# Both attentions of a two-layer diffusion block with the query halves in the two row halves of TensorE

## The chip, the core and the metric

The kernel runs on one core of a Trainium2 chip. The metric is the device time of one execution in microseconds. The kernel before takes 1738.92 us, the median of three runs (1737.24 to 1739.38). The profiled execution that all readings below come from spans 1736.6 us, 2.3 us less than that median. The names of engines in the profile: PE is TensorE's matmul, PEld its weight load, DVE VectorE, ACT ScalarE, POOL GpSimd, SP the engine that issues the transfers.

## The reference

Two layers work on 1024 latent tokens and 256 context tokens of width 1024. Each has an adaLN-modulated RMSNorm, an attention, a SiLU gate and an output projection. Layer 0 is grouped-query attention, 16 query heads of 64 on 4 key heads; layer 1 is latent attention, 16 heads whose query and key have 64 plain and 32 rotary dimensions, the rotary key shared by all heads. Cut to what matters here:

```
s = einsum('bqhgd,bkhd->bhgqk', q, k) * 64 ** -0.5          # layer 0
s = (einsum('bqhd,bkhd->bhqk', q_nope, k_nope)
     + einsum('bqhr,bkr->bhqk', q_rope, k_rope)) * 96 ** -0.5   # layer 1
p = softmax(s, axis=-1)
o = einsum('bhqk,bkhd->bqhd', p, v)
```

Latent queries see 1280 keys (1024 latent and 256 context). In layer 0 the context queries are computed too, over the 256 context keys; layer 1 gives out latent tokens only.

## The kernel before, in words

The program goes through layer 0's projections, layer 0's attention, its output projection with layer 1's norm, layer 1's projections, layer 1's attention, and its output projection. Everything that has to be exact is split into a high and a low part of the 4-byte type `F32R` (names ending in H and L, or A and B), and a product is a sum of high x high, low x high and high x low.

**An attention unit.** `Attention.run` goes over units, one head each (16 latent units in each layer; layer 0 also has four short units, one for the context queries of each key group). A unit has ten key tiles of 128 keys. For each key tile `do_scores` makes a score tile `st` of 128 keys x 1024 queries, in two matmuls of 512 queries for each product (line 422), and ACT takes its exponential into `p` (line 424). The unit ends with `do_av`, which multiplies `p` by the values with two matmuls side by side, one for each query half, in the two column halves of the array (line 458), and with `total`, the softmax sum, a matmul in four column quarters (line 500).

- Layer 0's scores are two products: `KA` (128 rows: the high key above the low key) with `QA` (the high query twice), and `KB` (64 rows of the high key and a row of -1) with `QB` (the low query and the row `crow` of maxima).
- Layer 1's are three: 96 rows of the high key with the low query, 96 of the low key with the high query, and 97 with the high parts of both and the row of maxima.

**The maxima.** The softmax subtracts a maximum per query. It is found ahead of the scores: for the unit after this one, 20 steps each make a tile `mx` of 128 queries x 512 keys with a matmul (16 steps with latent keys, kind "lat", one matmul of 512 columns at line 362; four steps with the context keys, kind "ctx", two of 256 columns at line 367 for two query tiles), and DVE reduces the tile (lines 363 and 369). After the 20th step `do_shift` reduces once more; its `turn` transposes the maxima on PE at the end of the running unit's scores, DVE copies them into `crow`, and SP sends them into the last row of the next unit's query tile. Two steps stand between the matmuls of each key tile. The first steps (28 in layer 0, 24 in layer 1) are made earlier, between the projection matmuls of the gate (`gate_slice`, lines 92 to 94).

**What sets the order.** In `run`, the instructions of PE, DVE and ACT stand in the order in which the code records them; POOL's and SP's are placed by the framework's scheduler. In the gate stage ahead of it, the scheduler places PE's too. PE's, DVE's and ACT's instructions start in the order of their queues. A tile is made again from a ring: `mx` has two PSUM banks, `st` two pairs of banks, `av` two. POOL adds up the `p` tiles for the softmax sum; DVE adds the last four in pairs (`pair_sum`, line 431) after the unit's scores.

## Time and profile before

| | |
|---|---|
| median of three runs | 1738.92 us |
| span of the profiled execution | 1736.6 us |
| PE busy | 1703.1 us (98%), 8548 matmul records |
| PEld busy | 1232.5 us (71%) |
| DVE busy | 1068.4 us (62%) |
| ACT, POOL busy | 644.5 us (37%), 979.5 us (56%) |
| TensorE clock granted | 0.997 |
| layer 0's attention, first score to last values | 367.9 to 763.3 us |
| layer 1's attention, first score to last sum | 1196.9 to 1645.0 us |

A busy time is the time in which at least one instruction of the engine ran. A matmul's own duration in the records is longer than the time it holds the array, since matmuls follow each other in a pipeline: what a matmul costs is the distance from its start to the next one's. In a timeline a row is a run of equal instructions: start, length, engine, line, what is written and read, shape, count, and in brackets the idle time before it with what ended it. The shape `96*128 96x512` is 96 rows and 128 columns of weights, and 512 columns that stream.

### The profile page before, as it was taken

The numbers are of one execution on the slowest core, as the hardware profiler recorded it, in microseconds if no ns is written. First come the engines' busy times: TensorE is split into PE (matmuls) and PEld (weight loads), VectorE is DVE, ScalarE is ACT, GpSimd is POOL, SyncE is SP. The second block draws the span as 40 slices with busy tenths as digits, with TensorE's granted clock in tenths as the row PEclk, the third lists the DMA queues.
The fourth block names the chain that finished last, engine by engine and source line by source line (L and its number), as shares of the span: only waits on it lengthen the run. The fifth ranks groups of instructions, "written<-read, shape, count | busy, mean of one in ns | idle before, by whom it ended". The sixth has DMA issues, their size and how long they took to land. (4 is left out here: it accounts for less than half of the span.)

```text
span 1736.6 us, 23794 instructions
## 1 busy us (share of the span) xinstructions
PE 1703.1 (98%) x8548; PEld 1232.5 (71%) x8548; DVE 1068.4 (62%) x1807; ACT 644.5 (37%) x943; POOL 979.5 (56%) x657
## 2 busy tenths in 40 slices
PE   8999999999999999999989999999999999999998
PEld 5776778776655665558878798978666666657587
DVE  3765651368777877625575667756676767667231
ACT  4632221134544544433244633332343443434310
POOL 2763430237888897752344644443587878777511
PEclk9999999999999999999999999999999999999999
DMA  9457854432332422156434857685434443441452
GB/s 326 156 160 235 265 167 136 133 98 55 100 91 71 116 66 74 44 145 189 137 94 132 238 163 199 181 234 162 104 88 118 108 104 91 111 112 43 118 162 73
DMA packets 211901, 234.33 MB, mean 135 GB/s; under 512 B 20680, under 2 KB 157880, under 8 KB 211784
## 3 DMA queue, kind: packets, MB, share of 16 engines
q1 hardware_dynamic: 211360, 232.71, 47.2%
q8 instruction: 67, 1.10, 0.3%
q14 instruction: 50, 0.41, 0.1%
q10 hardware_dynamic: 424, 0.11, 0.0%
HBM read 158.98 MB, written 73.63 MB: 134 GB/s over the span
## 5 line engine op out<-in xcount | busy, mean ns | idle before, releaser
L363 DVE TENSOR_REDUCE m<-mx 128x1 f32<-128x512 f32 x512 | 351.5, 691 | 203.6 <-PE mx L362 201.5
L424 ACT ACTIVATE p<-st 128x1024 f32<-128x1024 f32 x328 | 335.3, 1024 | 219.5 <-PE st L422 185.1
L445 POOL TENSOR_TENSOR acp<-acp,p 128x1024 f32<-128x1024 f32 x128 | 305.7, 2388 | 8.7
L458 PE MATMUL av<-p,v 128*64 128x512 f32 x1312 | 289.9, 595 | 0.0
L458 PEld LDWEIGHTS av<-p,v 128*64 128x64 f32 x1312 | 90.8, 137 | 181.0 <-issue 178.6
L445 POOL TENSOR_TENSOR acp<-p 128x1024 f32<-128x1024 f32 x34 | 81.3, 2391 | 168.3 <-ACT p L424 167.9
L445 POOL TENSOR_TENSOR acp<-acp,acd 128x1024 f32<-128x1024 f32 x60 | 141.5, 2358 | 22.2 <-DVE acd L431 19.4
L431 DVE TENSOR_REDUCE acd<-p 128x512 f32<-128x1024 f32 x124 | 144.6, 1219 | 7.7 <-ACT p L424 7.7
L135 POOL TENSOR_TENSOR wb<-wraw,wa 128x512 fp32r<-128x512 f32 (+3 forms) x73 | 95.5, 1324 | 90.6 <-ACT wa L156 90.0
L92 PE MATMUL mm<-wa,hh 128*128 128x512 f32 (+2 forms) x336 | 127.3, 379 | 1.7 <-ACT hh L787 1.7
L422 PE MATMUL st<-QH,KL 96*128 96x512 f32 x320 | 123.5, 392 | 0.0
L94 PE MATMUL mm<-wa,hl 128*128 128x512 f32 (+2 forms) x336 | 121.3, 361 | 1.4 <-DVE hl L790 1.4
L93 PE MATMUL mm<-wb,hh 128*128 128x512 f32 (+2 forms) x336 | 120.9, 360 | 0.0
L479 ACT COPY os<-av 128x512 f32<-128x512 f32 x36 | 21.1, 586 | 252.9 <-PE av L458 173.5
L369 DVE TENSOR_REDUCE m<-mx 128x2 f32<-128x512 f32 x144 | 99.3, 692 | 25.3 <-PE mx L367 24.4
L92 PE MATMUL y<-wa,oh 128*128 128x512 f32 (+1 forms) x296 | 114.1, 386 | 0.0
L93 PE MATMUL y<-wb,oh 128*128 128x512 f32 (+1 forms) x296 | 113.6, 384 | 0.0
L94 PE MATMUL y<-wa,ol 128*128 128x512 f32 (+1 forms) x296 | 113.6, 384 | 0.0
L422 PE MATMUL st<-QA,KA 128*128 128x512 f32 x336 | 106.6, 399 | 0.7 <-ACT p L424 0.7
L422 PE MATMUL st<-QB,KB 65*128 65x512 f32 x336 | 105.5, 395 | 0.0
L362 PE MATMUL mx<-KA,QA 128*128 128x512 f32 x256 | 102.4, 405 | 1.2 <-DVE m L363 1.0
L362 PE MATMUL mx<-KH,QH 96*128 96x512 f32 x256 | 102.3, 401 | 0.0
(232 smaller groups left out, 3423.4 us busy)
## 6 DMA issues: line engine op xcount, KB each, us to landing
mraw<-in_l_w_mod SPq DMA_DIRECT2D x64, 256.0 KB
wraw<-in_l_w_in SPq DMA_DIRECT2D x28, 512.0 KB
rb<-rrow SPq DMA_DIRECT2D x72, 128.0 KB
mraw<-in_l_w_mod SPq DMA_DIRECT2D x16, 512.0 KB
sgd<-gth SPq DMA_DIRECT2D x32, 256.0 KB
QA<-q0h SPq DMA_DIRECT2D x32, 256.0 KB
wraw<-in_l_w_out SPq DMA_DIRECT2D x16, 512.0 KB
sg<-sgd SPq DMA_DIRECT2D x64, 128.0 KB
```

Source lines behind the costliest of these rows:

```text
L92: pe.matmul(ps, lhsT=lh(k), rhs=rh(k), start=first and i == 0, stop=False)
L93: pe.matmul(ps, lhsT=lh(k), rhs=rl(k), start=False, stop=False)
L94: pe.matmul(ps, lhsT=ll(k), rhs=rh(k), start=False, stop=last and i == len(ks) - 1)
L135: eng.tensor_sub(lo, a, b)
L362: pe.matmul(m, lhsT=s["mq"][:, i * P:(i + 1) * P], rhs=s["mk"][:, n * 512:(n + 1) * 512], start=True, stop=True)
L363: dve.reduce_max(s["m"][:, i, n:n + 1], m, axis=AX.X)
L369: dve.reduce_max(s["m"][:, 2 * i:2 * i + 2, 2 if u["kind"] == "lat" else 0], m.rearrange("p (a b) -> p a b", a=2), axis=AX.X)
L422: pe.matmul(ps[:, n * 512:(n + 1) * 512], lhsT=lh, rhs=rf(n), start=(j == 0), stop=(j == len(prods) - 1))
L424: act.activation(p, ps, AF.Exp, scale=self.ops["scale"])
L431: dve.reduce_sum(t[:, ns], p2.rearrange("p a n -> p n a")[:, ns, :], axis=AX.X)
L445: pool.tensor_add(t, a, b)
L458: pe.matmul(s["av"][64 * n:64 * n + 64, :], lhsT=s["v"][:, kt, u["vc"]:u["vc"] + 64], rhs=p[:, n * 512:(n + 1) * 512], start=kt == kts[0], ...
```

## The change

`HALVES` switches both layers. The array's 128 rows are used as two halves of 64: every score and maximum matmul has at most 64 rows, and the first 512 queries' lie in rows 0 to 63, the last 512 queries' in rows 64 to 127. The keys are loaded twice, once into each half of the partitions; the query tiles become 128 x 512, with one query half in each half of the partitions.

- Layer 0's scores are four products for each query half (high key x high query, low key x high query, high key x low query, and a row of -1 with the row of maxima, in tiles that are zero elsewhere); a maximum is one product of 64 rows.
- Layer 1's scores are five for each half (high, low x high, high x low, the shared rotary key's high and low part with the high rotary query, and 33 rows with the low rotary query and the maxima); a maximum is two products, plain and rotary.
- `side_by_side` records the two halves' matmuls in turn, and `scores_by_halves` puts one maximum step of each half into every key tile: half 0's ahead of its products, half 1's in the middle of its own.
- `mx` gets three banks and `av` one, so `total` goes to an `mx` tile. Layer 1's low parts (`KL`, `QL`, `QS`) get two buffers and are loaded by `rest`, at the end of the unit two before; the tile `KS` is opened when layer 1's gate stage has ended; that stage's ring of gate tiles goes from four to two.

Three places in PE's order. First layer 1's scores, one key tile with latent maxima. Names are written<-streamed,weights. Before:

```order
L422 MATMUL st<-QH,KH 128x512 x2
L362 MATMUL mx<-KH,QH 128x512
L422 MATMUL st<-QL,KH 128x512 x2
L422 MATMUL st<-QH,KL 128x512
L362 MATMUL mx<-KH,QH 128x512
L422 MATMUL st<-QH,KL 128x512
```

and with the change, where the rows of the two halves take turns:

```order
L393 MATMUL mx<-KH,QH 128x512
L501 MATMUL st<-QH,KH 128x512
L393 MATMUL mx<-KR,QR 128x512
L501 MATMUL st<-QH,KL 128x512
L501 MATMUL st<-QH,KH 128x512
L501 MATMUL st<-QL,KH 128x512
L501 MATMUL st<-QH,KL 128x512
L393 MATMUL mx<-KH,QH 128x512
L501 MATMUL st<-QL,KH 128x512
L393 MATMUL mx<-KR,QR 128x512
L501 MATMUL st<-QR,KR 128x512 x2
L501 MATMUL st<-QS,KS 128x512 x2
```

Eight matmuls of the whole array for a key tile have become fourteen of half of it. Second, a key tile of layer 1 with context maxima, with the change:

```order
L403 MATMUL mx<-KH,QH 128x256
L403 MATMUL mx<-KR,QR 128x256
L403 MATMUL mx<-KH,QH 128x256
L403 MATMUL mx<-KR,QR 128x256
L501 MATMUL st<-QH,KH 128x512
L501 MATMUL st<-QH,KL 128x512
L501 MATMUL st<-QH,KH 128x512
L501 MATMUL st<-QL,KH 128x512
L501 MATMUL st<-QH,KL 128x512
L403 MATMUL mx<-KH,QH 128x256
L403 MATMUL mx<-KR,QR 128x256
```

The four matmuls of a context step stand in one piece, all in one half. Third, the maxima in layer 1's gate stage (the `mm` rows are the gate's). Before:

```order
L362 MATMUL mx<-KH,QH 128x512 x2
L92 MATMUL mm<-hh,wa 128x512
L93 MATMUL mm<-hl,wa 128x512
L94 MATMUL mm<-hh,wb 128x512
L362 MATMUL mx<-KH,QH 128x512
```

and with the change:

```order
L393 MATMUL mx<-KH,QH 128x512 x2
L393 MATMUL mx<-KR,QR 128x512 x2
L393 MATMUL mx<-KH,QH 128x512
L393 MATMUL mx<-KR,QR 128x512
L93 MATMUL mm<-hh,wa 128x512
L393 MATMUL mx<-KH,QH 128x512
L393 MATMUL mx<-KR,QR 128x512
L94 MATMUL mm<-hl,wa 128x512
```

The first two maxima stand side by side, the others alone between matmuls of the whole array. The diff, cut to its core:

```diff
+HALVES = (True, True)
...
-            self.ps_m = st.enter_context(tc.tile_pool(name=f"psm{l}", bufs=2, space=PSUM, side="right", reuse_waits="tile"))
+            self.ps_m = st.enter_context(tc.tile_pool(name=f"psm{l}", bufs=3 if HALVES[l] else 2, space=PSUM, side="right", reuse_waits="tile"))
+            if HALVES[l]:
+                self.ops["open"](self, st)
...
+            if l and HALVES[l]:
+                self.ops["open_late"](self, stp)
...
+                bufs = 1 if HALVES[l] and name == "ps_o" else 2
...
+        def max_parts(self, u, step):
+            s = self.state[id(u)]
+            kind, i, n = step
+            if kind == "lat":
+                half, spans = i // 4, [(i % 4, slice(n * 512, n * 512 + 512), slice(0, 512))]
+            else:
+                half, spans = i // 2, [(2 * (i % 2) + a, slice(NL, NT), slice(a * 256, a * 256 + 256)) for a in range(2)]
+            held = {}
+            def part(j):
...
+                q, k = pairs[j]
+                for t, ks, cs in spans:
+                    pe.matmul(held["m"][:, cs], lhsT=q[:, t * P:(t + 1) * P], rhs=k[:, ks], start=j == 0, stop=j == len(pairs) - 1)
+                if j == len(pairs) - 1:
+                    dve.reduce_max(s["m"][:, i, n:n + 1], held["m"], axis=AX.X)
+            def part_ctx():
...
+                for t, ks, cs in spans:
+                    for j, (q, k) in enumerate(pairs):
+                        pe.matmul(m[:, cs], lhsT=q[:, t * P:(t + 1) * P], rhs=k[:, ks], start=j == 0, stop=j == len(pairs) - 1)
...
+            if kind == "ctx":
+                return half, [part_ctx] + [lambda: None] * (self.ops["mparts"] - 1)
+            return half, [lambda j=j: part(j) for j in range(self.ops["mparts"])]
...
-                sp.dma_start(raw(s["crow"]), raw(r))
+                if HALVES[self.l]:
+                    for n in range(2):
+                        sp.dma_start(raw(s["crow"][n]), raw(r[4 * n:4 * n + 4, :]))
...
+        def side_by_side(*streams):
+            for t in range(max(map(len, streams))):
+                for stream in streams:
+                    if t < len(stream):
+                        stream[t]()
...
+        def scores_by_halves(self, u, kt, p, steps):
...
+            streams = [[lambda j=j, n=n: product(j, n) for j in range(last + 1)] for n in range(2)]
+            for half, parts in steps:
+                at_ = (last + 2) // 2 if half else 0
+                streams[half][at_:at_] = parts
+            self.side_by_side(*streams)
+            act.activation(p, ps, AF.Exp, scale=self.ops["scale"])
...
+                            if HALVES[self.l]:
+                                count += 2
+                                self.scores_by_halves(u, kt, ps[i], self.next_maxima(count, t + 1 + ahead))
...
+                        if end and t + 2 < self.started:
+                            self.state[id(self.units[t + 2])].pop("rest", lambda: None)()
...
+    def l0_maxima(s, n):
+        r = slice(64 * n, 64 * n + 64)
+        return [(s["QH"][r, :], s["KH"][r, :])]
...
+            return [(s["KH"][r, ks], s["QH"][r, :]), (s["KL"][r, ks], s["QH"][r, :]),
+                    (s["KH"][r, ks], s["QL"][r, :]), (s["minus"][r, :], s["X"][r, :])]
...
+    def l1_open_late(at, st):
+        at.KS = st.enter_context(tc.tile_pool(name="rope1s", bufs=1, reuse_waits="tile")).tile([P, NT], F32R, name="KS")
+        for n in range(2):
+            pool.memset(raw(at.KS[64 * n + 32:64 * n + 33, :]), -1.0)
+            sp.dma_start(raw(at.KS[64 * n:64 * n + 32, :]), kr1h)
...
+        def rest():
...
+            for b, cs in halves:
+                sp.dma_start(raw(KL[b:b + 64, :]), k1l[h // 2, r, :])
+                sp.dma_start(raw(QL[b:b + 64, :]), q1l[h, 0:64, cs])
+                sp.dma_start(raw(QS[b:b + 32, :]), q1l[h, 64:96, cs])
...
+    def l1_maxima(s, n):
+        r = slice(64 * n, 64 * n + 64)
+        return [(s["QH"][r, :], s["KH"][r, :]), (s["QR"][r, :], s["KR"][r, :])]
...
+            return [(s["KH"][r, ks], s["QH"][r, :]), (s["KL"][r, ks], s["QH"][r, :]), (s["KH"][r, ks], s["QL"][r, :]),
+                    (s["KR"][r, ks], s["QR"][r, :]), (at.KS[r33, ks], s["QS"][r33, :])]
...
-    with tc.tile_pool(name="wkg1", bufs=4, **right) as wkg:
+    with tc.tile_pool(name="wkg1", bufs=2 if HALVES[1] else 4, **right) as wkg:
```

More of the change, by code (lines that the diff above doesn't have):

```diff
@@ L411, in maxima, with product @@
                     self.do_shift(u)
+        def scores_by_halves(self, u, kt, p, steps):
+            s = self.state[id(u)]
+            ps = self.ps_s.tile([P, 1024], F32, name="st", tag="st")
+            prods = [self.ops["scores"](s, kt, n) for n in range(2)]
+            last = len(prods[0]) - 1
+            def product(j, n):
+                lh, rh = prods[n][j]
+                pe.matmul(ps[:, n * 512:(n + 1) * 512], lhsT=lh, rhs=rh, start=j == 0, stop=j == last)
+            streams = [[lambda j=j, n=n: product(j, n) for j in range(last + 1)] for n in range(2)]
[4 more added lines that the diff above has]
+            act.activation(p, ps, AF.Exp, scale=self.ops["scale"])
         def do_scores(self, u, kt, p, between):
@@ L496, in total @@
             def total():
-                t = s["av"] if u is not self.units[-1] else self.ps_m.tile([P, 512], F32, name="mx", tag="mx")
+                t = s["av"] if u is not self.units[-1] and not HALVES[l] else self.ps_m.tile([P, 512], F32, name="mx", tag="mx")
                 for i, part in enumerate(s["total"]):
@@ L1113, in l0_load @@
             KA = kp.tile([P, NT], F32R, name="KA", tag="KA")
-            KB = kp.tile([65, NT], F32R, name="KB", tag="KB")
-            sp.dma_start(raw(KA[0:64, :]), k0h[g // 2, r, :])
-            sp.dma_start(raw(KA[64:128, :]), k0l[g // 2, r, :])
-            sp.dma_start(raw(KB[0:64, :]), k0h[g // 2, r, :])
-            pool.memset(raw(KB[64:65, :]), -1.0)
+            KB = kp.tile([P if HALVES[0] else 65, NT], F32R, name="KB", tag="KB")
+            if HALVES[0]:
+                for t, src in ((KA, k0h), (KB, k0l)):
+                    for n in range(2):
+                        sp.dma_start(raw(t[64 * n:64 * n + 64, :]), src[g // 2, r, :])
+            else:
+                sp.dma_start(raw(KA[0:64, :]), k0h[g // 2, r, :])
+                sp.dma_start(raw(KA[64:128, :]), k0l[g // 2, r, :])
+                sp.dma_start(raw(KB[0:64, :]), k0h[g // 2, r, :])
+                pool.memset(raw(KB[64:65, :]), -1.0)
             at.kcache[g] = dict(KA=KA, KB=KB)
         KA, KB = at.kcache[g]["KA"], at.kcache[g]["KB"]
+        if HALVES[0]:
+            return l0_load_halves(u, at, lat, KA, KB)
         qp = at.qp if at.started % 4 < 3 else at.qp2
@@ L1156, in hybrid_kernel @@
         units.insert(pos, ctxu[g])
-    at = Attention(0, units, dict(scale=0.125, load=l0_load, scores=l0_scores, kbufs=2, qbufs=3, vw=256))
+    at = Attention(0, units, dict(scale=0.125, load=l0_load, scores=l0_scores, maxima=l0_maxima, mparts=1, open=l0_open, kbufs=2, qbufs=3, vw=256))
     stE = ExitStack()
@@ L1402, in hybrid_kernel @@
                               kts=list(range(TT))))
-    at = Attention(1, units, dict(scale=float(96 ** -0.5), load=l1_load, scores=l1_scores,
+    at = Attention(1, units, dict(scale=float(96 ** -0.5), load=l1_load, scores=l1_scores, maxima=l1_maxima, mparts=2, open=l1_open, open_late=l1_open_late,
                                   kbufs=3, qbufs=3, vw=128))
```

110 lines of the change are left out of this document (102 added, 8 removed).

## The prediction

> **What bounds the kernel now.** I read the page, the busy times of both attention stages, then PE's and DVE's timelines inside one unit of each layer.
>
> ```profile
> span 1736.6 us, 23794 instructions
> PE 1703.1 (98%) x8548; PEld 1232.5 (71%) x8548; DVE 1068.4 (62%) x1807; ACT 644.5 (37%) x943; POOL 979.5 (56%) x657
> ...
> 367.90:763.30 395.40, 394.08 (x1917) 235.19 (x1916) 298.69 (x439) 188.78 (x198) 321.29 (x156) 1.00 0.31 81
> 1196.90:1645.00 448.10, 448.10 (x2134) 287.62 (x2133) 293.21 (x421) 180.37 (x188) 324.43 (x161) 1.00 0.39 99
> ```
>
> In the two lower rows (window, then busy us of PE, PEld, DVE, ACT, POOL) PE never rests in either attention. So the number of PE slots should set the time, and a change that saves slots saves time, unless another engine stands just behind PE. That is decided inside a unit. Layer 1 first, PE's timeline:
>
> ```profile
> 1271.51 0.64 PE L500 MATMUL av<-acp,twos 128*32 128x256 f32 x8
> 1272.08 8.80 PE L458 MATMUL av<-p,v 128*64 128x512 f32 x40
> 1280.82 0.50 PE L362 MATMUL mx<-KH,QH 96*128 96x512 f32 x1
> 1281.15 0.62 PE L422 MATMUL st<-QL,KH 96*128 96x512 f32 x2
> 1281.62 0.40 PE L422 MATMUL st<-QH,KL 96*128 96x512 f32 x1
> ...
> 1292.05 0.41 PE L367 MATMUL mx<-KH,QH 96*128 96x256 f32 x2
> 1292.29 0.63 PE L422 MATMUL st<-QL,KH 96*128 96x512 f32 x2
> ...
> 1299.50 0.27 PE L382 MATMUL mx<-ident,m 128*8 128x128 f32 x1
> 1299.70 0.64 PE L500 MATMUL av<-acp,twos 128*32 128x256 f32 x8
> ```
>
> A unit lasts 1299.70 - 1271.51 = 28.19 us, of which scores and maxima take 1299.50 - 1280.82 = 18.68. Two matmuls of 512 columns from 1281.15 to 1281.62 give a **slot** of 0.233 us; two of 256 from 1292.05 to 1292.29 give 0.12 each. A unit has 60 score slots, 16 latent maxima and 8 context matmuls: 76 x 0.2325 + 8 x 0.12 = 18.63, which is the 18.68. So layer 1 is counted in slots.
>
> Layer 0's unit, PE and then DVE:
>
> ```profile
> 590.49 0.50 PE L362 MATMUL mx<-KA,QA 128*128 128x512 f32 x1
> ...
> 604.22 0.62 PE L422 MATMUL st<-QB,KB 65*128 65x512 f32 x2
> 604.68 0.27 PE L382 MATMUL mx<-ident,m 128*8 128x128 f32 x1
> 604.88 0.64 PE L500 MATMUL av<-acp,twos 128*32 128x256 f32 x8
> ...
> 591.03 5.66 DVE L363 TENSOR_REDUCE m<-mx 128x1 f32<-128x512 f32 x8 [4.22 <-PE mx L362]
> 596.71 2.83 DVE L369 TENSOR_REDUCE m<-mx 128x2 f32<-128x512 f32 x4
> 599.57 0.18 DVE L376 TENSOR_REDUCE m<-m 128x8 f32<-128x24 f32 x1
> 599.66 5.45 DVE L363 TENSOR_REDUCE m<-mx 128x1 f32<-128x512 f32 x8
> ...
> 1283.21 0.69 DVE L363 TENSOR_REDUCE m<-mx 128x1 f32<-128x512 f32 x1 [0.23 <-PE mx L362]
> 1284.13 0.69 DVE L363 TENSOR_REDUCE m<-mx 128x1 f32<-128x512 f32 x1 [0.23 <-PE mx L362]
> ```
>
> From 591.03 to 599.66 + 5.45 = 605.11 DVE reduces without a gap: 14.08 us for 20 maxima and one small reduce, while PE's phase runs from 590.49 to 604.88, 14.39 us. In layer 0 two engines are full at once. In layer 1 (last two rows) DVE rests 0.23 us before every reduce.
>
> **The change part by part.** First the price p of a **pair**, two matmuls of 64 rows, one in each half. No row of the trace has one. The floor is one slot, 0.2325. The ceiling is two slots, 0.465, if the halves take turns. The nearest rows are the column halves:
>
> ```profile
> 238.03 0.39 PE L94 MATMUL mm<-wa,hlc 128*128 128x512 f32 x1
> 238.35 1.02 PE L214 MATMUL tp<-modrow,fold 128*2 128x512 f32 x2
> 239.30 0.50 PE L92 MATMUL mm<-wa,hhc 128*128 128x512 f32 x1
> 239.64 0.40 PE L93 MATMUL mm<-wb,hhc 128*128 128x512 f32 x1
> ```
>
> One lone 4-byte matmul of 512 columns (two passes, two records) takes 239.30 - 238.35 = 0.95, of which 0.09 is the change of shape (below): 0.86. The 20 column pairs of the values take 1280.82 - 1272.08 = 8.74, less 0.09: 0.43 for two records, 0.86 for a whole pair. There, two cost what one costs. A row pair also needs two weight loads per slot; the 256-column rows show one load and one matmul every 0.12, so two loads one after the other need 0.24. I take p = 0.236, between 0.2325 and 0.24. The Trainium skill ("TensorE: Matmul & The Clock Gate", Part 3) gives the span of row tiles as one matmul and about 4 ns for each further tile; by it p would be 0.2365 and the sum 0.5 us worse. No run here shows it yet.
>
> Second, **the change of shape**. From the last product at 238.03 to the next row is 0.32 where a slot is 0.23: 0.09 more. The first product after it keeps PE 239.64 - 239.30 = 0.34, 0.10 more, since its weights weren't loaded ahead. So a change costs 0.19 to 0.20, and a stretch of another shape between full-array products costs about 0.4. The trace changes columns only; for rows I take the same, with 0 as the other end. The Trainium skill ("TensorEngine Tiling (Array Packing)", Tiling Modes, Key Properties) says that changing the tiling mode drains the engine, which the 0.09 agrees with, and it doesn't exempt rows.
>
> *Layer 1's units.* A key tile with latent maxima goes from eight slots to seven pairs (five products, two parts of a maximum). Eight such tiles cost 8 x 7 x 0.236 = 13.2. In the two tiles with context maxima, half 0's four matmuls of 256 stand in one piece: PE starts in its queue's order, so the first product of half 1 starts after three of them, 0.36 us late, with its half idle; half 1's own four do the same to half 0. Placing the 18 rows of such a tile in order gives 2.12 us where seven pairs would be 1.63, so 2 x (7 x 0.236 + 0.49) = 4.3; about 0.1 is lost where the halves end apart. Sum 17.6 against 18.68: -1.08. 320 - 24 = 296 maxima lie in units, two to a key tile: 148 tiles, or 14.8 units: -16.0. The last 12 tiles, without maxima, go from 6 slots to 5 pairs: 12 x (1.18 - 1.395) = -2.6. **-18.6 us.** Without loss by queue order it would be -33.
>
> *Layer 0's units.* Scores go from four slots to four pairs, maxima from two slots to one pair per key tile; PE needs only 50 x 0.236 = 11.8 us. But the 20 reduces stay, at 0.68 to 0.69 each (5.45/8, 2.83/4). `mx` has three banks, and the turn and `total` now take one each before the values begin, so `total` waits for the 19th reduce. First reduce 0.54 after the unit's start (591.03 - 590.49), 19 x 0.69 and 0.1 for the small one: 13.75, where `total` starts at 14.39 now. **The stall that was PE's becomes DVE's**, and only -0.6 is left, in 14 whole units: **-8.4.** Ends: 0, and -10.5 with reduces at 0.68. The four short units and the last key tiles count nothing. This also hides p up to 13.75/50 = 0.275.
>
> *The gate stages.* In layer 1 the 24 early maxima now have two products each, and only the first two of a group of six are paired: placing the rows gives about 40.6 slots instead of 24, +3.9; 15 stretches between full-array products at 0.4: +6.0. Together **+9.9** (+3.9 if a change of rows is free). In layer 0, seven groups of four become three together and one alone, three slots for four, -1.6, and 14 stretches, +5.6: **+4.0** (-1.6).
>
> *Layer 1's start.* `KS` may be written only when the last gate product has been read. Two memsets and two transfers follow, and SP has the last gate tile's store between these:
>
> ```profile
> 1196.68 0.39 PE L94 MATMUL mm<-hh,wb 128*128 128x512 f32 x1
> ...
> 1197.95 0.68 DVE L302 SCALAR_TENSOR_TENSOR gth<-gth,mm 128x512 f32<-128x512 f32 x1
> 1198.65 0.34 SPq L303 DMA_DIRECT2D sgd<-gth  x1
> ...
> L1384 POOL MEMSET KH<- 1x1280 f32 x16 | 18.5, 1160 | 7.2 <-issue 3.5 <-PE mx L382 3.1
> ```
>
> The memsets end 2 x 1.16 after that product; the store issues at 1198.65, 1.7 us after its end (0.23 from 1196.68), so the second transfer starts near +2.1 and lands, by my estimate from these gaps, near +4. The first `KS` product stands after six pairs, +1.4 to +1.6. **+2.4**, once (0 to 4).
>
> *Transfers.* Per unit of layer 1 SP issues `KL`, `QL`, `QS` for two units later, six transfers, ahead of the two `crow` ones; the fifth score product waits for `crow`.
>
> ```profile
> 1271.50 0.46 SPq L1382 DMA_DIRECT2D KH<-k1h  x1
> ...
> 1271.50:1275.50 4.00, 4.00 (x25) 1.36 (x26) 3.88 (x5) 1.02 (x1) 3.33 (x3) 1.00 0.76 215
> ```
>
> Six issues at 0.46 are 2.8 us; 1.05 MB at 215 GB/s, the loads' rate now, 4.9. Their sum is 7.7 if nothing overlaps, and cover is 0.57 + 8.74 + five pairs, 10.5. Nothing is counted; without that cover each microsecond is paid 15 times. The duplicated keys and the removed `KH` memsets lie beside work in the same way.
>
> **Sum:** -18.6 - 8.4 + 9.9 + 4.0 + 2.4 = -10.7 against the span's 1736.6. The median is 2.3 above that execution, so 1738.9 - 10.7 = **1728 us**.
>
> **The rivals.**
>
> 1. *A pair costs more than a slot*, because the two weight loads or the two streams get in each other's way: slower. Layer 1 has 1100 pairs, so each 1 ns of p costs 1.1 us, and the gain is gone at 0.236 + 10.7/1100 = 0.246. This one mechanism decides the sign. With the halves fully in turn, p = 0.465, layer 1 pays 1100 x 0.229 = 252 and layer 0 (50 x 0.465 - 13.75) x 14 = 133, with 13 in its last tiles: 1728 + 398 = 2126 us. At p = 0.26 it is 1728 + 26 = 1754. For it: a load is recorded at 188 ns, and two of those exceed a slot; against it: the 0.12 rhythm and the column pairs.
>
> ```profile
> L422 PEld LDWEIGHTS st<-QH,KL 96*128 96x128 f32 x320 | 60.1, 188 | 12.4
> ```
>
> 2. *Queue order costs less, or shape changes in rows are free*: without the loss in context tiles layer 1 gives -33 instead of -18.6, with free changes the gate stages give 11.6 back: 1728 - 14 - 12 = 1702. For it: nothing in the trace has row halves. Against it: every timeline I read starts in program order.
> 3. *The losses around the units eat the gain*: pairs at 0.242 and the upper ends of start and `crow` (a microsecond late in half the units): 1728 + 6.6 + 1.6 + 7.5 = 1744, which begins at no change.
>
> **How the numbers follow.** Forecast, a moderate gain with its sum between -4 and -28: 0.52. Rival 2 beyond that, down to 1695: 0.10. Rival 1 from 0.249 on: 0.20, of which half lies beyond 1800. Rival 3, near no change or a little over: 0.18. No change is within 0.2%, 3.5 us, about what a measurement of this kernel can tell. Faster: 0.52 + 0.10 = 0.62; same: two thirds of rival 3, 0.12; slower: 0.20 + 0.06 = 0.26. Low end 1700, rival 2 nearly whole; high end 1754, p = 0.26 in layer 1. The likeliest case's own range is 1711 to 1735.
>
> **What would show it.** Right: in layer 1 two score rows of the two halves start within some 0.12 us of each other and the next pair 0.236 later; units of 27.0 to 27.2 us; context tiles of 2.1 us against 1.65. In layer 0 units of about 23.0, DVE's reduces without a gap, and `mx` matmuls that wait for DVE. In the gate stages lone maxima with 0.2 us around them; one wait of about 2 us for `KS`. Wrong: starts 0.23 apart within a pair (rival 1), layer 0's units near 21.6 (DVE didn't bound), a wait for `crow` in each unit, or context tiles as short as the others.

## The result, and the profile after

The changed kernel takes **1708.95 us** (median of four runs, 1707.59 to 1711.43), the kernel before 1738.47 (1737.24 to 1739.38) beside it: a ratio of 0.9832, 95% interval 0.9818 to 0.9846. That is 29.5 us less, where 10.7 less was forecast. The time lies in the predicted range (1700 to 1754) and the sign is right; the size is off by a factor of almost three, so some terms of the sum were wrong.

The page of the kernel after, its first lines, and its two attention stages by busy time (window, length, busy us of PE, PEld, DVE, ACT, POOL, then clock and transfers):

```profile
span 1705.8 us, 27449 instructions
PE 1667.9 (98%) x10244; PEld 1196.9 (70%) x10244; DVE 1046.6 (61%) x1807; ACT 645.1 (38%) x943; POOL 961.4 (56%) x646
...
371.90:750.00 378.10, 375.38 (x2586) 207.98 (x2587) 277.72 (x437) 188.08 (x198) 319.20 (x154) 1.00 0.27 74
1196.90:1613.00 416.10, 414.41 (x3118) 278.20 (x3122) 291.40 (x419) 180.38 (x187) 310.01 (x149) 1.00 0.53 124
```

PE is as full as before, on 20% more matmul records; the span is 30.8 us shorter. To place that, I split both executions where a unit's product with the values begins: the first and the last unit of layer 0, the first and the last of layer 1. In the timeline of PE of the kernel before these rows start at 381.05, 761.95, 1215.69 and 1638.55; in the kernel after:

```profile
384.35 1.08 PE L555 MATMUL av<-p,v 128*64 128x512 f32 x4
...
748.98 1.94 PE L555 MATMUL av<-p,v 128*64 128x512 f32 x8
...
1215.47 1.08 PE L555 MATMUL av<-p,v 128*64 128x512 f32 x4
...
1607.86 1.51 PE L555 MATMUL av<-p,v 128*64 128x512 f32 x6
```

| stretch | before | after | measured | predicted |
|---|---|---|---|---|
| up to layer 0's first values (its gate stage) | 381.05 | 384.35 | +3.3 | +4.0 |
| layer 0's units | 380.9 | 364.6 | **-16.3** | -8.4 |
| up to layer 1's first values (its gate stage and start) | 453.7 | 466.5 | +12.8 | +9.9 + 2.4 |
| layer 1's units | 422.9 | 392.4 | **-30.5** | -18.6 |
| sum | | | -30.7 | -10.7 |

The two cost rows came out within a microsecond of the forecast, but in part because they are cut at the values: each also holds the scores of its layer's first unit, and those got shorter too. Cut at the first score, layer 0's gate stage cost 3.9 us (first score at 367.97 before, at 371.91 after). Layer 1's gate stage, from its first product to its first score, went from 50.7 to 62.2 us. Of these 11.4 more, 0.98 is a wait that belongs to the start of the units, so the gate stage cost 10.5 where 9.9 was forecast. The start cost 2.6 in two waits where 2.4 was forecast. The first unit gave back 1.6: from its first score to its values it takes 18.53 for 18.55, in spite of the 1.60 of the second wait. Another 1.3 us lies ahead of the gate stage, in work that the change leaves alone, and within the scatter of the runs (that stretch takes 383.2 to 387.1 us in them). With its first unit, layer 1 gave 32.1 us.

Both gains inside the units were about 1.6 to 2 times what I had worked out. A whole unit (from one unit's first value product to the next one's, median) goes from 23.61 to 22.45 us in layer 0 and from 28.19 to 26.12 in layer 1.

**Layer 1.** PE's timeline in the kernel after, some latent rows first, then the start of a key tile with context maxima:

```profile
1277.02 0.39 PE L501 MATMUL st<-QL,KH 64*128 64x512 f32 x1
1277.03 0.39 PE L501 MATMUL st<-QH,KH 64*128 64x512 f32 x1
1277.26 0.39 PE L393 MATMUL mx<-KH,QH 64*128 64x512 f32 x1
1277.26 0.39 PE L501 MATMUL st<-QH,KL 64*128 64x512 f32 x1
...
1286.34 0.28 PE L403 MATMUL mx<-KH,QH 64*128 64x256 f32 x1
1286.35 0.49 PE L501 MATMUL st<-QH,KH 64*128 64x512 f32 x1
1286.46 0.28 PE L403 MATMUL mx<-KR,QR 64*128 64x256 f32 x1
1286.58 0.28 PE L403 MATMUL mx<-KH,QH 64*128 64x256 f32 x1
...
1286.70 0.28 PE L403 MATMUL mx<-KR,QR 64*128 64x256 f32 x1
```

Two things are to be seen. The two halves' rows start within 0.01 us of each other and the next pair 0.23 later (1277.03, 1277.26): a pair costs one slot. And at 1286.35 half 1's product starts 0.01 us after half 0's first context matmul, though three more of half 0's matmuls (1286.46, 1286.58, 1286.70) stand ahead of it in PE's order. So what is said ahead of the prediction, that PE's instructions start in the order of their queue, holds within one row half, not between the two. A context tile takes 1.65 us (1286.34 to the next at 1287.99), not the 2.12 that I had placed by hand.

**Layer 0.** DVE's, ACT's and PE's rows in one scoring phase of the kernel after; the brackets give the idle time ahead of a row and what ended it:

```profile
674.93 4.99 DVE L395 TENSOR_REDUCE m<-mx 128x1 f32<-128x512 f32 x8 [4.25 <-PE mx L393]
...
677.03 0.18 PEld L501 LDWEIGHTS st<-QH,KA 64*128 64x128 f32 x2 [0.25 <-ACT p L508]
...
678.55 2.11 ACT L508 ACTIVATE p<-st 128x1024 f32<-128x1024 f32 x2 [0.50 <-PE mx L393]
...
679.63 0.19 PEld L501 LDWEIGHTS st<-QH,KA 64*128 64x128 f32 x2 [0.23 <-ACT p L508]
...
682.24 0.18 PEld L501 LDWEIGHTS st<-QH,KA 64*128 64x128 f32 x2 [0.44 <-ACT p L508]
```

DVE reduces without a gap, as predicted, but eight reduces take 4.99 us, 0.62 each, not 0.69. And PE's first score of every second key tile (677.03, 679.63, 682.24) waits for ACT: the score tile has two buffers, and the one to be written is still read by the exponential. I had not named this wait at all.

### The profile page after: what moved, and what is told of

Same layout as the page of the kernel before. It is cut to its first block, busy times and chain, and to the rows that moved or that the text cites. A ratio compares the mean times of both kernels' runs of the same rounds, so it can differ in the third digit from the quotient of the medians.

```text
span 1705.8 us, 27449 instructions
## 1 busy us (share of the span) xinstructions
PE 1667.9 (98%) x10244; PEld 1196.9 (70%) x10244; DVE 1046.6 (61%) x1807; ACT 645.1 (38%) x943; POOL 961.4 (56%) x646
## 5 line engine op out<-in xcount | busy, mean ns | idle before, releaser
L395 DVE TENSOR_REDUCE m<-mx 128x1 f32<-128x512 f32 x512 | 336.2, 687 | 176.3 <-PE mx L393 170.5
L501 PE MATMUL st<-QH,KH 64*128 64x512 f32 x320 | 122.2, 404 | 1.0 <-DVE gth L303 1.0
L501 PE MATMUL st<-QH,KL 64*128 64x512 f32 x320 | 119.0, 392 | 0.0
L501 PE MATMUL st<-QL,KH 64*128 64x512 f32 x320 | 118.3, 390 | 0.0
L576 ACT COPY os<-av 128x512 f32<-128x512 f32 x36 | 21.1, 587 | 255.9 <-PE av L555 205.9
L404 DVE TENSOR_REDUCE m<-mx 128x2 f32<-128x512 f32 x144 | 95.4, 688 | 24.0 <-PE mx L403 18.9
L393 PE MATMUL mx<-KH,QH 64*128 64x512 f32 x256 | 102.7, 405 | 0.5 <-DVE m L404 0.3
L93 PE MATMUL mm<-hh,wa 128*128 128x512 f32 x256 | 102.0, 399 | 0.5 <-ACT th L86 0.5
```

Source lines behind the costliest of these rows:

```text
L93: pe.matmul(ps, lhsT=lh(k), rhs=rh(k), start=first and i == 0, stop=False)
L393: pe.matmul(held["m"][:, cs], lhsT=q[:, t * P:(t + 1) * P], rhs=k[:, ks], start=j == 0, stop=j == len(pairs) - 1)
L395: dve.reduce_max(s["m"][:, i, n:n + 1], held["m"], axis=AX.X)
L404: dve.reduce_max(s["m"][:, 2 * i:2 * i + 2, 2 if u["kind"] == "lat" else 0], m.rearrange("p (a b) -> p a b", a=2), axis=AX.X)
L501: pe.matmul(ps[:, n * 512:(n + 1) * 512], lhsT=lh, rhs=rh, start=j == 0, stop=j == last)
```

## The experiments

All times are compared with 1738 to 1739.6, which the kernel before takes beside them, and with the 1709 of the kernel after.

### One layer alone

```
-HALVES = (True, True)
+HALVES = (False, True)
```

This is layer 1 alone; `(True, False)` is layer 0 alone. Layer 1 alone:

> Only layer 1 works by halves of the rows; layer 0 is as in the kernel before. Theory A (the stages of the two traces add up: layer 1's units gave 30.5 us, its gate stage and start took 12.8): 1738.5 - 17.7 = 1720.8, within 2 us, with a layer-1 period of 26.1. Theory B (the terms of the prediction: 18.6 given by layer 1's units, 12.3 taken): 1738.5 - 6.3 = 1732.2, with a period of 27.0 to 27.2. If the parts lean on each other (a stage of layer 1 gains only because layer 0 ends otherwise), the two runs of one layer do not add up to the whole of -29.5.

Layer 0 alone:

> Only layer 0 works by halves; layer 1 is as before. Theory A (the stages add up: layer 0's units gave 16.4 us, its gate stage took 3.4): 1738.5 - 13.0 = 1725.5, within 2 us, with a layer-0 period of 22.4. Theory B (the terms of the prediction: 8.4 given, 4.0 taken): 1738.5 - 4.4 = 1734.1, with a period of 23.0.

Measured: layer 1 alone 1724.39 us (1721.88 to 1726.90; ratio 0.9921, 0.9906 to 0.9936), layer 0 alone 1726.81 (1726.24 to 1727.35; 0.9936, 0.9919 to 0.9952). Both lie nearer to the stages' sum than to the terms of the prediction, and the units are those of the kernel after within 0.01 (392.4 us for layer 1's, 22.46 for one of layer 0's). But 13.6 and 11.2 make 24.8, not 29.5. In the profiled executions the spans are 12.7 and 12.1 us shorter, against 30.8, and the 6.0 that are missing there lie in one place, layer 1's gate stage of the run with layer 1 alone: from its first product to the first score it takes 68.2 us, in the kernel after 62.2. A row of the view of waits is longer there, and the busy times by stretch show what followed it (length, busy us of the five engines, granted clock):

```profile
PE mx L393 <- DMA QH<-q1h: 1.6, 1, 1.6
...
1168.00:1171.00 3.00, 1.36 (x7) 0.68 (x5) 0.00 (x0) 0.00 (x0) 0.00 (x0) 1.00 1.01 205
...
1174.00:1178.00 4.00, 4.00 (x8) 1.63 (x7) 1.38 (x2) 0.47 (x1) 0.00 (x0) 0.50 0.96 268
```

PE got to the first unit's queries 1.6 us before they had landed; in the kernel after it is 0.2. After that pause the granted clock is 0.50 until about 1182, and eight matmuls take 4 us. So the layers are independent in their units, and what does not add up is a pause for a transfer and a slow clock behind it.

### Does TensorE start in the order of its queue?

```
-            self.side_by_side(*streams)
+            if self.l:
+                for f in streams[0] + streams[1]:
+                    f()
+            else:
+                self.side_by_side(*streams)
```

In layer 1 half 0's seven matmuls of a key tile are now recorded first, then half 1's.

> Layer 1's key tiles write all matmuls of the upper half one after the other, then all of the lower half, seven each; nothing else changes. Theory of the prediction (TensorE starts matmuls in the order of its queue): the halves hardly overlap, a key tile takes 14 slots of 0.2325 = 3.26 us in place of 1.63, a unit of ten key tiles about 16 us more, 16 units about 260 us: near 1970. Theory of the trace after (a half takes its next matmul as soon as it is free, past waiting ones of the other half, as at 1286.34): no change, 1709 within 5, if it can look ahead seven matmuls. A look-ahead of some matmuls only lies between: the start of the lower half's first score, counted in slots of the upper half, tells how many.

Measured: 1734.08 us in one execution, 25 us more than the kernel after where strict order would have cost 260; layer 1's unit is 27.73. Its timeline on PE, where all seven matmuls of a tile's half 0 (the second `mx` of the row at 1290.12 is the first, `st<-QS,KS` at 1291.65 the last) stand ahead of its half 1 (from 1291.06):

```profile
1290.12 0.55 PE L393 MATMUL mx<-KH,QH 64*128 64x512 f32 x2
1290.36 0.54 PE L393 MATMUL mx<-KR,QR 64*128 64x512 f32 x2
...
1290.74 0.39 PE L501 MATMUL st<-QH,KH 64*128 64x512 f32 x1
...
1290.96 0.39 PE L501 MATMUL st<-QH,KL 64*128 64x512 f32 x1
1291.06 0.41 PE L501 MATMUL st<-QH,KH 64*128 64x512 f32 x1
1291.19 0.39 PE L501 MATMUL st<-QL,KH 64*128 64x512 f32 x1
...
1291.42 0.39 PE L501 MATMUL st<-QR,KR 64*128 64x512 f32 x1
```

Both halves work all the time. Half 1's first product starts at 1291.06, when four of half 0's seven have started and three (1291.19, 1291.42 and one at 1291.65) still wait ahead of it; the other half's tile is caught at its end in the same way. The halves stay four slots apart, and a tile takes (27.73 - 26.12)/10 = 0.16 us more. TensorE does start matmuls of one row half past waiting ones of the other, here past three.

### What sets layer 0's unit: VectorE's reduces or the score buffers?

First the reduces alone. The latent maxima are taken over 256 of the 512 key columns and the exponential's factor is a quarter, so the softmax is another one; TensorE's and ScalarE's work is the same.

```
-                    dve.reduce_max(s["m"][:, i, n:n + 1], held["m"], axis=AX.X)
+                    dve.reduce_max(s["m"][:, i, n:n + 1], held["m"] if self.l else held["m"][:, :256], axis=AX.X)
...
```

> Layer 0's latent maxima are taken over 256 of the 512 key columns of each product, and its exponential's factor is a quarter so that nothing overflows; so the softmax is not the reference's, while TensorE's and ScalarE's work is the same. Theory (layer 0's scoring phase is bound by VectorE: 20 reduces at about 0.62 us against some 11.7 us of TensorE): reduces halve, the phase falls from 13.15 to TensorE's 11.7, a unit from 22.4 to 21.0, sixteen latent units by about 23 us: 1686 to 1692. Rival (layer 0's phase is bound by TensorE, the reduces only follow it): no change, 1709 within 3.

Measured: 1705.60 us in one execution; layer 0's unit is 22.45, the same as with whole reduces. My theory falls: DVE's rows show no gap in the kernel after, but it does not set the period. The view of PEld's waits within layer 0's units names what does. Kernel after (us in total, times, longest):

```profile
PEld st L501 <- ACT p L508: 20.7, 61, 0.7
```

With the short reduces:

```profile
PEld st L501 <- ACT p L508: 20.7, 62, 0.7
```

The wait is the same to the tenth. So the next run shortens the time that a score buffer is held, by putting the maximum's product ahead of the scores in both halves:

```
-                at_ = (last + 2) // 2 if half else 0
+                at_ = (last + 2) // 2 if half and self.l else 0
```

> Layer 0 only: in each half the maximum's product stands ahead of the four score products of the key tile, where before the lower half had it behind its second. The run with half-length reduces left layer 0's period at 22.45, so VectorE is not what sets it. Theory (the loop through the two score buffers sets it: a tile's first score at 677.03 waits for ScalarE's exponential of the tile two before, and its own exponential starts 1.52 us later and takes 1.05; two tiles in 2.60): with the maximum outside, the span from first score to exponential loses one slot of 0.2325, the loop falls to 2.37 for two tiles, 1.18 each, but VectorE's two reduces of about 0.62 then set 1.25; a unit of ten tiles goes from 22.45 to about 21.9, sixteen units give 7 to 9 us: 1700 to 1702. Rival (VectorE's two reduces set the period, as the prediction had it): no change, 22.45 and 1709 within 2.

Measured: layer 0's unit is 21.95 (21.9 was expected), its stage 5.3 us shorter than in the kernel after. The wait for ACT is nearly gone, and now a wait for DVE stands in its place, PEld's waits again:

```profile
PEld mx L393 <- DVE m L395: 6.7, 31, 0.3
...
PEld st L501 <- ACT p L508: 2.4, 5, 0.7
```

The whole kernel is at 1705.26 (1701.21 to 1708.57; 0.9801, 0.9781 to 0.9821): the wide spread is taken up below. Both edits together:

> The maximum's products first, as in the run before, and the short reduces too (layer 0's latent maxima over 256 of 512 columns and a quarter of the exponential's factor, so not the reference's softmax). Theory of the two score buffers: with VectorE out of the way the tile falls to TensorE's five slots of 0.2325 = 1.16, at most the loop's 1.18; the period is 21.1 to 21.3, sixteen units give 18 to 20 us against the 1705.6 of the short reduces alone: near 1687. Rival (neither buffers nor VectorE set it, TensorE's own pace does): the period stays at 22.45.

Measured: 21.61 for a unit, 1704.73 us in one execution. 21.1 to 21.3 was a slip in the expectation: ten tiles of 1.17 and the 9.9 of turn, sum and values are 21.6, which the prediction had named as the mark of "DVE didn't bound". That is TensorE's own pace or close to it: five slots of 0.2325 are 1.16 a tile, and a wait for ACT's score buffers is back (8.4 us in 30 times in the view of PEld's waits), so these two can't be told apart here. So layer 0's unit has limits close together: TensorE at 21.6 or just below, VectorE at most 0.35 above that, the two score buffers of the kernel after 0.5 higher still. The kernel after sits on the third. The whole of this execution gains almost nothing over the run before: the granted clock fell to 0.50 from 557.7 to 561.1 and from 1151.6 to 1161.8, and in two places PE waits for POOL's sum of `p`, 4.3 us in all, 2.8 in the run before and 0.7 in the kernel after. A faster layer 0 runs into POOL there.

Is VectorE's 0.35 to be had by moving reduces? One pair of maxima of each unit goes ahead of the product with the values, on top of the maxima first:

```
-                                count += 2
+                                held_back = not self.l and t and group[0] == kts[0] and i == 0 and len(self.units[t - 1]["kts"]) > 4
+                                count += 0 if held_back else 2
...
+                        if not self.l and end and whole and not final:
+                            count += 2
+                            self.maxima(count, t + 1 + ahead)
                         self.do_av(u, group, ps)
```

> The maximum's products first, and in layer 0 one pair of maxima of each latent unit is moved from the first key tile of the next unit to the place ahead of the unit's product with the values, where VectorE has 4.25 us of rest; 18 in place of 20 reduces are left in the scoring phase. If VectorE is what is left of the bound once the maxima stand first, the phase loses 2 x 0.62 = 1.24 less what TensorE's pace leaves (ten tiles of 1.16 to 1.18), and TensorE pays one more change of shape, 0.2: a period of 21.5 to 21.7 and 4 to 7 us less than the run with the maxima first, so 1694 to 1698. If it is not, the change of shape alone remains: 2 to 3 us more than that run.

Measured: 1712.29 us (1711.24 to 1717.41; 0.9852, 0.9836 to 0.9867), 7 us worse than without. The usual unit is 22.10, 0.15 above: from its first score to `total` it takes 0.3 less (12.37 for 12.66), so relieving VectorE does give that, but from `total` to the values 0.42 more (0.99 for 0.57), the early pair with its change of shape there and back. And three units take about 25. In two of them (waits of DVE in the first, then of PE over the whole stage):

```profile
DVE crow L424 <- DMA shift<-crow: 2.7, 1, 2.7
```

```profile
PE mx L393 <- DVE crow L424: 4.1, 2, 2.0
```

Two `turn`s fall into one unit, `crow` has one buffer, so the second copy waits for the transfer of the first, and the early pair on PE waits behind it on DVE. The third stands right behind the first of these waits and ran at a granted clock of 0.50 from 432.4 to 439.2. A dead end, with a known cause.

### What the gate stage costs, and whether it can be had back

In the kernel after most early maxima stand alone in their half. PE's timeline there:

```profile
1158.71 0.50 PE L93 MATMUL mm<-hh,wa 128*128 128x512 f32 x1
1159.14 0.49 PE L393 MATMUL mx<-KH,QH 64*128 64x512 f32 x1
1159.48 0.39 PE L393 MATMUL mx<-KR,QR 64*128 64x512 f32 x1
1159.80 0.49 PE L94 MATMUL mm<-hl,wa 128*128 128x512 f32 x1
```

From 1159.14 to 1159.80 one maximum takes 0.66 us, two slots and 0.20; the first gate product behind it takes 0.42 to the next stretch at 1160.22. The next run writes PE's order out, with pairs of maxima between a slice's eight steps of three products:

```
...
-            gate_slice(1, c, m, s0, 512, (wg, wg1)[c], hT, ps_mm, wkg)
-            if 2 < at.step < len(todo_g) - 1:
-                at.maxima(at.done + 6, 2)
+            def pair(k):
+                if k in (1, 4, 7) and 2 < at.step < len(todo_g) - 1:
+                    at.maxima(at.done + 2, 2)
+            with in_order(mybir.EngineType.PE):
+                gate_slice(1, c, m, s0, 512, (wg, wg1)[c], hT, ps_mm, wkg, pair)
...
```

> Layer 1's gate stage alone: TensorE's order is written out there, with a pair of maxima (one per half) behind the second, fifth and eighth of a slice's eight steps, so that nearly all maxima have a partner. In the trace after, the maxima took 13.66 us of that stage in 17 stretches, most of them alone in their half. Theory of the prediction (a lone maximum costs its two slots of 0.2325 and the changes of shape 0.2; paired it shares both): 12 pairs, 24 slots or 5.6 us, and about twelve changes, 2.4: 8.0, so 5 to 6 us less: 1703 to 1704. Rival (the stage waits for its transfers and for the reduces, not for TensorE's slots: the transfers of the first unit's queries arrive as late as before): less than 2 us, 1707 to 1709.

Measured: 1707.26 us (1706.98 to 1708.22; 0.9818, 0.9803 to 0.9832), 1.7 less than the kernel after. From the first matmul of a stretch of maxima to the next gate product there are now 9.98 us in all for 13.66, but PE comes earlier to the first unit's queries:

```profile
PE mx L393 <- DMA QH<-q1h: 2.6, 2, 2.1
```

Slots saved in front of a late transfer become a wait. The first score still comes 1.3 us earlier in its stage (60.85 from the first product, for 62.16), but in this execution the granted clock was 0.50 from 1196.6 to 1203.4, at the start of layer 1's units, and the first unit takes 21.28 us up to its values instead of 18.53. So the 1.7 isn't a clean measure of the pairs, and the maxima have to start later too. First that alone, on top of layer 0's maxima first:

```
-            if 2 < at.step < len(todo_g) - 1:
-                at.maxima(at.done + 6, 2)
+            if 3 < at.step < len(todo_g) - 1:
+                at.maxima(at.done + 8, 2)
```

> Layer 0 with the maximum's products first, and in layer 1's gate stage the maxima begin one slice (5.6 us of gate products) later, eight to a slice for three slices in place of six for four. In the run with the maxima first alone layer 0 gave the 5.3 us, but the time spread from 1701.2 to 1708.6 with the mean granted clock from 0.998 to 0.994, and in the profiled execution the gate stage was 3.8 us longer: TensorE waited 0.8 us for QH<-q1h at 1152.9 and ran at a granted clock of 0.50 from 1157 to 1163. Theory (that wait sets off the slow clock): without the wait the gate stage stays at a clock of 1.00 and at 62 us, the times lie close together at 1701 to 1703. Rival (the slow clock comes from the half-filled array of the lone maxima, not from the wait): it falls to 0.50 here too, and the time spreads as before around 1705.

Measured: 1704.53 us (1701.13 to 1706.57; 0.9803, 0.9787 to 0.9819). The execution with the profile is the fastest, 1701.13: no wait for `QH`, a clock of 1.00 through the stage. But the others are 1.8 to 5.4 us slower at mean granted clocks of 0.993 to 0.999, which are not in the order of their times. So the spread did not go away, neither theory accounts for it, and it stays open. The later start with all maxima in pairs (`k in (1, 3, 5, 7)` and `3 < at.step`):

> As the run before it, and TensorE's order in layer 1's gate stage written out, each maximum with its partner in the other half behind the second, fourth, sixth and eighth step of three slices. In the run with paired maxima alone the time in their stretches fell from 13.66 to 9.98, and 2.5 us of waiting for QH<-q1h gave most of it back. Theory of the prediction (a lone maximum pays its slots and its changes of shape): with nothing to wait for, the 3.7 us come through, or up to 5.6 with all pairs whole: 1696 to 1699. Rival (the stage is held by the reduces, six to eight of them behind three buffers): no gain over the run before it.

Measured: **1694.96 us** (1694.56 to 1698.27; 0.9748, 0.9734 to 0.9763). The gate stage, first product to first score, goes from 62.66 in the run before it to 56.01, the stretches of maxima from 13.68 to 8.01, which is the 8.0 that 24 slots and twelve changes of shape make. The time is below the 1696 to 1699 expected, and not all of the 9.6 us between the two medians is the pairs': the profiled executions are 6.3 apart, which the gate stage accounts for, and the rest is the open spread of the run before it. A stretch in it:

```profile
1153.49 0.40 PE L95 MATMUL mm<-hh,wb 128*128 128x512 f32 x1
1153.82 0.50 PE L393 MATMUL mx<-KH,QH 64*128 64x512 f32 x2
1154.15 0.40 PE L393 MATMUL mx<-KR,QR 64*128 64x512 f32 x2
1154.48 0.51 PE L93 MATMUL mm<-hh,wa 128*128 128x512 f32 x1
1154.83 0.40 PE L94 MATMUL mm<-hl,wa 128*128 128x512 f32 x1
```

Each of the four steps from 1153.49 to 1154.83 is 0.33 to 0.35 where a slot is 0.23: 0.41 for one change into row halves and one back.

The last two terms. `KS` on two queues:

```
-            sp.dma_start(raw(at.KS[64 * n:64 * n + 32, :]), kr1h)
+            (sp, act)[n].dma_start(raw(at.KS[64 * n:64 * n + 32, :]), kr1h)
```

> As the run before it, and the second half of KS is fetched on ScalarE's queue in place of SyncE's, where it stood behind the last store of the gate (issued at 1197.31 where the first half was issued at 1195.57). Theory of the prediction (layer 1's start waits for KS: 1.6 us at 1200.2): 1.5 us less than the run before it, 1694.5 to 1697.5, and the wait for KS gone; the wait of 1.0 for the last gate product's bank stays. Rival (the wait is for the bandwidth, not for the issue): the same time as the run before it.

In the kernel after, the two transfers and the score that waits for them:

```profile
1195.57 0.33 SPq L1529 DMA_DIRECT2D KS<-kr1h  x1
...
1196.92 0.34 SPq L304 DMA_DIRECT2D sgd<-gth  x1
...
1197.31 0.42 SPq L1529 DMA_DIRECT2D KS<-kr1h  x1
...
1200.19 0.47 PE L501 MATMUL st<-QS,KS 33*128 33x512 f32 x1 [1.60 <-DMA KS<-kr1h]
```

and with the second one on ACT's queue:

```profile
1184.34 0.37 ACTq L1529 DMA_DIRECT2D KS<-kr1h  x1
...
1187.67 0.47 PE L501 MATMUL st<-QS,KS 33*128 33x512 f32 x1 [0.15 <-DMA KS<-kr1h]
```

Measured: 1694.83 us (1693.73 to 1697.60; 0.9746, 0.9731 to 0.9760). The wait is gone from its place, 1.60 to 0.15, so it was the order on SP's queue; in the median of the whole kernel the 1.5 us can't be told from nothing.

At last layer 0's gate stage in pairs too, behind the third and sixth step of a slice:

```
...
+                def pair(k):
+                    if k in (2, 5) and (m or s0 == 1024) and (m, s0) != (3, 1024):
+                        at.maxima(at.done + 2, 2)
...
```

> All of the run before it, and TensorE's order written out in layer 0's gate stage too, with a pair of maxima (one per half) behind the third and the sixth step of each slice. In the trace after, the maxima took 10.39 us of that stage in 19 stretches of one or three. Theory of the prediction (a lone maximum pays its slot and its change of shape): 14 pairs of 0.2325, 3.3, and 14 changes of 0.2, 2.8, make 6.1, so 3 to 4 us less than 1694.8: 1690.5 to 1692. Rival (stretches of three already share their slots, and more stretches cost more changes): within 1 us of 1694.8.

Measured: 1695.12 us (1693.09 to 1696.71; 0.9752, 0.9739 to 0.9765): no gain. The stretches there sum to 10.87 us, not 6.1, of which a new wait is 2.1, and there are 19 stretches for the 14 counted.

```profile
PE mx L393 <- DMA KA<-k0h: 2.1, 1, 2.1
```

As in layer 1, the earlier place runs into a transfer that has not landed, and the granted clock was 0.50 from 315.3, the end of that wait, to 322.1. So this run doesn't tell what the pairs are worth there. A later start wasn't tried.

## Why the prediction was right or wrong, point by point

- **The price of a pair: right.** 0.236 was taken from bounds of 0.2325 and 0.24; the rows give 0.23 from pair to pair, at the floor. Rival 1 (a pair dearer than a slot, the slower side) falls: the two weight loads and the two streams do not get in each other's way. Over 1100 pairs the difference to 0.236 is 3 to 4 us of gain that I left out.
- **Layer 1's units: wrong, -18.6 for -30.5 (-32.1 with the first unit).** The step that failed is "PE starts in its queue's order, so the first product of half 1 starts after three of them". It starts 0.01 us after the first. With the seven matmuls of a half in one block TensorE still overlaps the halves. The two context tiles take 1.65 us each, not 2.14 (7 x 0.236 + 0.49): 0.98 of the 0.99 us by which a unit's gain was off (-2.07 for -1.08); the smaller p gives 0.2 more, and about as much is lost elsewhere in the phase. The figure "without loss by queue order it would be -33" stood in the prediction; I gave its case, rival 2, 0.10. The reason, "every timeline I read starts in program order", came from timelines without row halves. The Trainium skill ("TensorE: Matmul & The Clock Gate", Part 3) also has matmuls start and end strictly in program order; for two different row halves the rows at 1286.35 and 1291.06 show otherwise.
- **Layer 0's units: wrong, -8.4 for -16.3.** The step that failed is "the stall that was PE's becomes DVE's", with 19 x 0.69 = 13.1. Two errors stand in it, of opposite sign. The spacing of 0.68 to 0.69 in the kernel before was not DVE's own: free of PE, reduces follow each other after 0.62, while each is still recorded with 0.687. With that the phase would have been 12.4. (The end of -10.5 for reduces at 0.68 is a slip too: 14 times 0.79 is 11.1.) And a third limit was missed, the loop through the two score buffers: 1.52 us from a tile's first score to its exponential and 1.05 for that, 2.60 for two tiles. It holds the phase at 13.15 where I had 13.75. The sign I had named for it, DVE without a gap, does stand in the trace after, and still it was not the cause: halving the reduces changed nothing, moving half 1's maximum ahead of its scores gave 0.5 us a unit. Records that are longer than the spacing hide short rests: the reduces from 674.93 on start 0.60 to 0.61 apart, but 0.70 and 0.80 at single places.
- **The gate stages: right.** Up to the first score +3.9 for +4.0 in layer 0, and +10.5 for +9.9 in layer 1. The lone maxima with 0.2 on either side are in the timeline, and pairing layer 1's gave back what the terms say they cost, once they started later; in layer 0 that isn't shown.
- **Layer 1's start: right in cause, a little small.** A wait of 1.60 for `KS`, because the second transfer stands behind the last gate tile's store on SP, as worked out; another of 0.98 stands ahead of it, for the bank of that gate tile, which I had not named. Together they are 2.6 for the 2.4.
- **Transfers: right.** In the units one score of layer 0 waits 0.3 us for its maxima, and none in layer 1.
- **Rival 2** (1702) came nearest: its queue order was right, its free change of shape was not. **Rival 3** fell with rival 1's price; what is real in it is the first unit's queries landing late, 0.2 us in the kernel after, and 1.6 us with a slow clock behind it in the run with layer 1 alone.

## What to carry to other kernels

Work on disjoint row halves of the array as on two queues: place them so that each is always fed, and don't charge one with the other's place in the order, at least for a few matmuls. An engine without a gap is a suspect, not a bound: before summing its durations, look at what the row ahead of it waits for, and follow each small ring (here two score buffers) once around. And slots saved just ahead of a transfer that lands late are not saved: move the work behind the transfer first; here the pairs gave 1.7 us without that, and with it 6.3 less than the same start unpaired in the profiled executions (9.6 in the medians); that version, at 1695 us, beats both kernels.

## What the runs showed of the hardware that was not expected

- Matmuls of different row halves start out of program order: past three waiting ones of the other half (1286.35, 1291.06). How far it would go beyond three wasn't tried.
- A pair of 64-row matmuls of 512 columns with a weight load each goes at 0.23 us, as one matmul of 128 rows does, with both loads hidden. A change between whole rows and halves costs as a change of columns does, 0.41 us there and back.
- VectorE's reduces of 128x512 follow each other after 0.62 us though each is recorded with 0.687.
- The granted clock fell to 0.50 for some 10 us behind a wait of 1.6 us (run with layer 1 alone), and for some 7 us behind one of 0.8 us (maxima first), both between lone half-array matmuls:

```profile
1153.00:1155.00 2.00, 1.26 (x6) 1.00 1.00 206
...
1157.00:1159.00 2.00, 2.00 (x5) 0.50 1.04 296
```

These are of the run with the maxima first (length, busy us of PE, granted clock). After the 2.1 us of wait with paired maxima it stayed at 1.00. At layer 1's start, where PE waits 0.98 and then 1.5 to 1.7 us in nine of the traces, it stayed at 1.00 in seven, the kernel after among them, and fell to 0.50 in two (short reduces, paired maxima). The Trainium skill ("TensorE: Matmul & The Clock Gate", Part 1) has the clock go down to half after an idle window of about 3.4 us. That agrees with the one long pause of PE in every trace, 4.6 to 6.2 us near 870 to 890 us, in or behind which the clock fell to 0.50 for 3.4 to 6.8 us. But it fell with waits of 0.8 to 2.1 us too, so the length of one pause doesn't settle it. Whether the half-filled array ahead of it matters stays open.
